# Gate projections of a hybrid decoder layer: tile by tile, and by Strassen's scheme on pairs of column tiles with three of four weight sums made by adding transfers

## The chip, the cores and the metric

The kernel runs on one core of one Trainium2 chip. A core has a matrix engine (TensorE, PE in the profile), a vector engine (VectorE, DVE), a scalar engine (ScalarE, ACT), a general engine (GpSimd, POOL) and a queue engine (SyncE, SP), each with its own instruction stream; transfers run on 16 DMA engines. PE takes a 128x128 weight block and streams columns of the other operand past it; results go to PSUM, eight banks of 128 x 512 fp32. All other tiles lie in SBUF. The metric is device time in microseconds (us); lower is better. Before: 1664.61 us, the median of 3 runs (1664.39 to 1665.62).

## What is computed

One decoder layer on 512 tokens of width 2048, in float32, no batch:

```python
h = rmsnorm(x) * (1 + scale) + shift                  # scale, shift, gate from c @ w_ada
q_lat, kv_lat, k_rope, z_mla, u, v, z_sgu, g_mla, g_sgu = split(h @ w_in)
A = causal_attention(from q_lat, kv_lat, k_rope) * silu(z_mla)
B = u * (tril(W_s) @ rmsnorm(v) + b_s) * silu(z_sgu)   # chunks of 128 tokens
x = x + gate * ((sigmoid(g_mla) * A + sigmoid(g_sgu) * B) @ w_out)
out = rmsnorm(x)
```

The change is about the five projections of width 2048 that gate the two branches: z_mla, g_mla, u, z_sgu, g_sgu, here called types z, g, u, s, t. Each has 16 column tiles of 128, one per head.

## The kernel before

Every product of two fp32 matrices is made of three float32r matmuls: each operand is split into a high part (`hi`, a cast on ACT) and a low part (`lo`, a subtraction on DVE), and `mm3` (L133 to L136) adds hi*hi, hi*lo and lo*hi into one PSUM bank. The input h stands transposed in SBUF as 16 chunks of 128 rows by 512 tokens, as pairs `hh[j]`, `hl[j]`.

Weights come through one `Stream` (L53): granules of up to 128 x 1024 are loaded into three raw buffers in a fixed order (L76, on SP's queue), then split into one of two `whi`/`wlo` pairs (L97 on ACT, L98 on DVE) one granule ahead of their use. Every engine runs its instructions in the order in which the program is written, so the order of the Python calls is the schedule.

The stages, in order: the modulation vectors and the first 1664 columns of the projection (latents, and three gate tiles of head 15 among them); v (L466); the gate projections of heads 0 to 14 (L749); the last two gate tiles of head 15 (L814); attention head by head (L1008); the output projection (L1068).

In the gate stage each head h has five tiles t, each with two granules of eight chunks: 16 chunks of three matmuls over all 512 tokens. After a tile, `evac` (L693) applies the gate from PSUM. Beside that run the spatial mix of v (`sgu_prep`, `sgu_mix`) for the first eight h, the sums that carry `shift` into the early projections (`shift_share`), the rotary tables (`rope_part`, one small step before each granule) and the norms of the latents. The gate results of all 32 tiles stay in SBUF until attention uses them.

## Time and profile before

| | |
|---|---|
| median of 3 runs | 1664.61 us |
| profiled execution, its own time | 1664.88 us |
| its span | 1663.2 us |
| mean granted TensorE clock | 0.999 |
| waits of PE that the profile shows, all together | 3.7 us (1.6 + 1.1 + 0.8 + 0.2) |
| data moved | 228.63 MB, 137 GB/s over the span |

The span is what the profile sees between the first and the last instruction. A PE row's duration is not its cost: matmuls overlap, so the cost of one in a stream is the distance between the starts of two neighbours. Rows of DVE and ACT do not overlap with others of the same engine; their durations add up.

### The profile page before, as it was taken

The page shows a single profiled execution, that of the slowest core. Times are in us where ns is not written, and L with a number is a line of the kernel's source. Part 1 is how long each engine was busy: PE and PEld are TensorE (multiplying, and loading weights), DVE is VectorE, ACT ScalarE, POOL GpSimd, SP SyncE. Part 2 cuts the span into 40 slices and gives each one's busy share as a digit, 9 for nine tenths or more (in the row PEclk, how much of TensorE's full clock was granted, in tenths as well). Part 3 has the DMA queues.
Part 4 walks back from the last instruction along what each step waited for, and adds up shares of the span by engine and source line. Part 5 has one row for each costly group of instructions (what it writes and reads, how often), then busy time and mean ns, then how long its engine had stood idle before and what let it go on. Part 6 is the DMA issues. An engine that isn't in the chain of part 4 may idle for free.

```text
span 1663.2 us, 20082 instructions
## 1 busy us (share of the span) xinstructions
PE 1651.6 (99%) x8024; PEld 1406.1 (85%) x8024; DVE 947.5 (57%) x1456; ACT 583.3 (35%) x967; POOL 2.2 (0%) x11
## 2 busy tenths in 40 slices
PE   9999999999999999999999999999999999999998
PEld 7888889988888888888888888888898888888887
DVE  8988646365665644444443533323578778874453
ACT  4343333234223322221223322222455555542332
POOL 0000000000000000000000000000000000000000
PEclk9999999999999999999999999999999999999999
DMA  9878557344444333322222222232311221126332
GB/s 379 346 295 303 193 211 269 101 151 143 142 152 132 120 137 127 123 102 89 98 92 102 89 101 100 90 102 81 96 61 58 63 75 55 61 77 253 127 101 101
DMA packets 64508, 228.63 MB, mean 137 GB/s; under 512 B 7304, under 2 KB 9376, under 8 KB 57632
## 3 DMA queue, kind: packets, MB, share of 16 engines
q1 hardware_dynamic: 64416, 227.37, 38.7%
q8 instruction: 62, 1.02, 0.2%
q14 instruction: 30, 0.25, 0.0%
HBM read 223.14 MB, written 4.20 MB: 137 GB/s over the span
## 4 chain that ended last, share of the span: by engine, by line
PE 98%; DMA 1%; DVE 0%; ACT 0%; issue 0%; SPq 0%; DVEq 0%
PE ps L135 32%; PE ps L134 32%; PE ps L136 32%; PE ps L947 1%; PE ps L675 1%; PE ps L910 1%; PE ps L911 1%; DMA wraw<-in_w 1%; PE ps L676 0%; DMA wada<-in_c 0%; PE ps L606 0%; DVE wlo L98 0%; ACT whi L97 0%; PE ps L446 0%; DVE wada L122 0%
## 5 line engine op out<-in xcount | busy, mean ns | idle before, releaser
L98 DVE TENSOR_TENSOR wlo<-wraw,whi 128x1024 fp32r<-128x1024 f32 (+3 forms) x304 | 339.0, 1115 | 577.4 <-ACT whi L97 566.4
L134 PE MATMUL ps<-hh,whi 128*128 128x512 f32 x1640 | 641.6, 391 | 0.2 <-ACT hh L389 0.2
L135 PE MATMUL ps<-hl,whi 128*128 128x512 f32 x1640 | 638.5, 389 | 0.8 <-DVE hl L125 0.8
L136 PE MATMUL ps<-hh,wlo 128*128 128x512 f32 x1640 | 638.4, 389 | 0.0
L97 ACT CAST whi<-wraw 128x1024 fp32r<-128x1024 f32 (+3 forms) x304 | 293.7, 966 | 801.6 <-PE ps L135 561.0
L136 PEld LDWEIGHTS ps<-hh,wlo 128*128 128x128 f32 x1640 | 307.8, 188 | 64.5 <-DVE wlo L98 0.2
L135 PEld LDWEIGHTS ps<-hl,whi 128*128 128x128 f32 x1640 | 308.0, 188 | 64.0 <-DVE hl L125 1.1
L134 PEld LDWEIGHTS ps<-hh,whi 128*128 128x128 f32 x1640 | 307.9, 188 | 63.7 <-ACT hh L389 0.6
L134 PE MATMUL ps<-whi,hh 128*128 128x512 f32 (+3 forms) x448 | 148.9, 332 | 0.0
L135 PE MATMUL ps<-wlo,hh 128*128 128x512 f32 (+3 forms) x448 | 148.6, 332 | 0.1
L136 PE MATMUL ps<-whi,hl 128*128 128x512 f32 (+3 forms) x448 | 148.5, 332 | 0.0
L125 DVE SCALAR_TENSOR_TENSOR wada<-wada,cact 128x2048 f32<-128x2048 f32 x47 | 107.2, 2281 | 1.2 <-DMA wada<-in_wada 1.2
L135 PEld LDWEIGHTS ps<-wlo,hh 128*128 128x128 f32 x448 | 84.6, 189 | 5.4 <-DVE wlo L98 0.4
L136 PEld LDWEIGHTS ps<-whi,hl 128*128 128x128 f32 x448 | 84.6, 189 | 5.0
L134 PEld LDWEIGHTS ps<-whi,hh 128*128 128x128 f32 x448 | 84.6, 189 | 5.0
L134 PE MATMUL ps<-whi,b 128*128 128x512 f32 (+1 forms) x212 | 81.8, 386 | 0.0
L135 PE MATMUL ps<-wlo,b 128*128 128x512 f32 (+1 forms) x212 | 81.6, 385 | 0.0
L136 PE MATMUL ps<-whi,g 128*128 128x512 f32 (+1 forms) x212 | 81.6, 385 | 0.0
L134 PEld LDWEIGHTS ps<-whi,b 128*128 128x128 f32 x212 | 39.8, 188 | 7.9
L135 PEld LDWEIGHTS ps<-wlo,b 128*128 128x128 f32 x212 | 39.8, 188 | 7.9
L136 PEld LDWEIGHTS ps<-whi,g 128*128 128x128 f32 x212 | 39.8, 188 | 7.9
L139 ACT CAST lat<-ps 128x512 fp32r<-128x512 f32 (+1 forms) x64 | 35.4, 570 | 13.4 <-PE ps L136 13.3
(229 smaller groups left out, 1340.8 us busy)
## 6 DMA issues: line engine op xcount, KB each, us to landing
wraw<-in_wh SPq DMA_DIRECT2D x150, 512.0 KB, 3.3
wada<-in_wada SPq DMA_DIRECT2D x47, 1024.0 KB, 5.9
wraw<-in_w SPq DMA_DIRECT2D x32, 512.0 KB, 3.5
wraw<-in_wo SPq DMA_DIRECT2D x32, 512.0 KB, 3.3
wraw<-in_w SPq DMA_DIRECT2D x32, 320.0 KB, 2.9
wraw<-in_wv SPq DMA_DIRECT2D x16, 512.0 KB, 3.2
wraw<-in_wv SPq DMA_DIRECT2D x16, 384.0 KB, 3.3
wraw<-in_wq SPq DMA_DIRECT2D x16, 384.0 KB, 2.9
```

Source lines behind the costliest of these rows:

```text
L97: self.nc.scalar.copy(hi[:, :n], raw[:, :n])
L98: self.nc.vector.tensor_tensor(out=lo[:, :n], in0=raw[:, :n], in1=hi[:, :n].bitcast(F32), op=ALU.subtract)
L125: DVE.scalar_tensor_tensor(out=out, in0=in0, scalar=scalar, in1=in1, op0=op0, op1=op1, **kw)
L134: PE.matmul(ps, ah, bh, start=start, stop=False)
L135: PE.matmul(ps, ah, bl, start=False, stop=False)
L136: PE.matmul(ps, al, bh, start=False, stop=stop)
L139: ACT.copy(hi, src)
L675: PE.matmul(ps[:, n2], vh[:, n, :], whl[:, q], start=True, stop=False)
L910: PE.matmul(ps, q2[:, q], krh[:, :n], start=False, stop=False)
L911: PE.matmul(ps, q2[:, q], krl[:, :n], start=False, stop=True)
L947: PE.transpose(ps[:, o:o + P], pr_[i][:, j * P:(j + 1) * P], ident)
```

## The change

The gate projections of 76 of the 77 tiles (all of heads 0 to 13, and of 14 and 15 what is left) are computed in 38 pairs of column tiles (`PAIRS`) by Strassen's scheme in Winograd's form. A pair is a 2x2 block problem: the two halves of the 2048 rows of weights, the two column tiles, and the two halves of the 512 tokens. It takes seven products of eight chunks, each over 256 columns, where two tiles took eight such block products (as 16 chunks over 512 columns, twice). One tile (type z, head 14) is still made plainly.

* Sums of the activations (`s1`, `s2`, `s4`) are made once, during the stage of v; `s3` replaces the right half of `hh[0..7]`, `hl[0..7]` at the start of the gate stage.
* Of a pair's four quarters of weights, called 11, 12, 21 and 22, four sums are needed: 11 += 12 by DVE, then 11 += 22, 12 += 22 and 11 += 21 by transfers from DRAM that add into SBUF, issued on POOL's queue. In the first and the last pair DVE makes one and three of these.
* Each product has its own split into `hi` and `lo`, two products ahead, into one of three buffers. The program is a list of slots, one product each; other work is attached to a slot with `on(slot, phase, ...)`.
* The memory that all this needs is freed by writing v, the latents and the 32 gate results to DRAM and fetching them later: the results during attention (`fetch`, 32 loads of 128 x 512), before the key weights of each head.
* The same side work as before (mix, shift sums, latents, rotary tables) runs inside the slots. Two row sums become one plain fp32 matmul each. PSUM banks are named instead of taken in turn.

```diff
+PAIRS = [((t, h), (t, h + 1)) for h in range(0, 14, 2) for t in TYPES]
+PAIRS[5:5] = [(("g", 14), ("u", 14))]
+PAIRS += [((t, 14), (t, 15)) for t in "st"]
...
+    def make_s12(j):
+        a, b = (nt(tb.p, [P, S], F32, f"t{i}") for i in range(2))
+        tt(a, hh[j].bitcast(F32), hl[j].bitcast(F32), ALU.add)
+        tt(b[:, right], hh[j + 8].bitcast(F32)[:, right], hl[j + 8].bitcast(F32)[:, right], ALU.add)
+        tt(b[:, right], a[:, right], b[:, right], ALU.subtract)
+        split_sum("s1", j, b[:, right])
+        tt(b[:, left], b[:, right], a[:, left], ALU.subtract)
+        split_sum("s2", j, b[:, left])
...
+    for i in range(13):
+        early.setdefault(8 + i, []).append(lambda i=i: lat_scale(i))
+    for j in range(8):
+        early.setdefault(11 + 2 * j + j // 2, []).append(lambda j=j: make_s12(j))
+        early.setdefault(32 + j, []).append(lambda j=j: make_s4(j))
...
+            turn_ = [(1, k), (6, k), (3, k - 1), (7, k), (4, k - 1), (5, k), (2, k)]
...
+    def transfer(t, k, q, add):
+        ty, h = PAIRS[k][q % 10 - 1]
+        eng = dict(accum_op=ALU.add) if add else {}
+        q_ = nc.gpsimd if add else DMA
...
+        if h < H - 1:
+            q_.dma_start(t, wh[h, n, q // 10 - 1], **eng)
+            return
...
+        on(at_[6] - 2, GATE, add, k, 11, 12)
+        for p, q, r, ready in ((2, 11, 22, at_[6]), (3, 12, 22, at_[6]), (4, 11, 21, at_[2])):
+            if acc_[p]:
+                on(ready - 1, LOAD, lambda k=k, q=q, r=r: transfer(raws[k, q], k, r, True))
+            else:
+                on(at_[p] - 2, GATE, add, k, q, r)
...
+    def make_s3(j):
+        a = slot(("rx", "lat12")[j % 2])
+        tt(a, hh[j].bitcast(F32), hl[j].bitcast(F32), ALU.add)
+        tt(a[:, left], a[:, left], a[:, right], ALU.subtract)
+        hilo(hh[j][:, right], hl[j][:, right], a[:, left])
+    for j in range(8):
+        on(-2 + j * 2 // 3, BACK, make_s3, j)
...
+    for i in range(0, len(rope), 2):
+        on(s_ + 4 + i // 2, BACK, lambda i=i: [f() for f in rope[i:i + 2]])
...
-                for k in range(8):
-                    j = half * 8 + k
-                    sl = slice(k * P, (k + 1) * P)
-                    mm3(ps, wH[:, sl], wL[:, sl], hh[j], hl[j], j == 0, j == KC - 1)
...
+    for s, (p, k) in enumerate(order):
+        if s > 0:
+            evacuate(*order[s - 1], s)
+        run(s, FIRST, EVAC, GATE, SPLIT, BACK)
+        begin(p, k)
+        ps, rt_, (wH, wL) = bank_for(p, k), rights[p], split_of.pop(s)
+        for c in range(8):
+            xh, xl = rt_(c)
+            sl = slice(c * P, (c + 1) * P)
+            st, sp = c == 0 and p in (1, 5, 6), c == 7
+            PE.matmul(ps, wH[:, sl], xh, start=st, stop=False, skip_group_check=True)
+            PE.matmul(ps, wH[:, sl], xl, start=False, stop=False, skip_group_check=True)
+            PE.matmul(ps, wL[:, sl], xh, start=False, stop=sp, skip_group_check=True)
+        run(s, MISC, LOAD)
```

How the instructions stand on the engines, at the three places that matter below. First PE, in the middle of the gate stage before (`whi`, `wlo`: a granule's split weights; `hh`, `hl`: the chunks):

```order
L134 MATMUL ps_4983<-hh_173_1384,whi_4950 128x512
L135 MATMUL ps_4983<-hl_175_1388,whi_4950 128x512
L136 MATMUL ps_4983<-hh_173_1384,wlo_4951 128x512
L134 MATMUL ps_4983<-hh_183_1431,whi_4984 128x512
L135 MATMUL ps_4983<-hl_185_1435,whi_4984 128x512
L136 MATMUL ps_4983<-hh_183_1431,wlo_4985 128x512
```

and with the change, where one product ends and the next begins (`s4h`, `s4l`: a sum of activations; `w0`, `w2`: two of the three split buffers):

```order
L1159 MATMUL ps_588_5145<-s4h_2709,w0h_5141 128x256
L1160 MATMUL ps_588_5145<-s4l_2710,w0h_5141 128x256
L1161 MATMUL ps_588_5145<-s4h_2709,w0l_5142 128x256
L1159 MATMUL ps_547_4845<-hh_184_1460,w2h_5172 128x256
L1160 MATMUL ps_547_4845<-hl_186_1464,w2h_5172 128x256
L1161 MATMUL ps_547_4845<-hh_184_1460,w2l_5173 128x256
```

A split of 128 x 1024 now serves 24 matmuls of 256 columns instead of 24 of 512.

Second DVE, where the rotary tables are made; before (`wlo`: low part of a granule; `rb` to `rs`: the table's steps; `acc`: the shift sums):

```order
L98 TENSOR_TENSOR wlo_3147<-wraw_3040,whi_3146 128x1024
L125 SCALAR_TENSOR_TENSOR acc_277_2869<-wraw_3034,shift_91,acc_277_2869 128x1024
L129 TENSOR_SCALAR rd_3155<-rb_2950 128x128
L131 TENSOR_SCALAR re_3157<-rd_3155 128x128
L122 TENSOR_TENSOR rd_3155<-rd_3155,re_3157 128x128
L122 TENSOR_TENSOR rs_3046<-rs_3046,rd_3155 128x128
L98 TENSOR_TENSOR wlo_3187<-wraw_3097,whi_3186 128x1024
```

and with the change (`w0l`, `w2l`: low parts of two successive products; `lat`: a result being gathered from PSUM; `rx`, `cosT`: the table's steps):

```order
L123 TENSOR_TENSOR lat_1251_10439<-lat_1251_10439,ps_1245_10376 128x256
L123 TENSOR_TENSOR w0l_10709<-raw_1259_10528,w0h_10708 128x1024
L130 TENSOR_SCALAR rx_10530<-rx_10530 128x128
L132 TENSOR_SCALAR rx_10530<-rx_10530 128x128
L123 TENSOR_TENSOR rx_10530<-rx_10530 128x128 x2
L130 TENSOR_SCALAR rx_10530<-cosT_10531 128x128
L132 TENSOR_SCALAR rx_10530<-rx_10530 128x128
L123 TENSOR_TENSOR rx_10530<-rx_10530 128x128 x2
L123 TENSOR_TENSOR w2l_10747<-raw_1242_10366,w2h_10746 128x1024
```

Before, one step of the table stands between two splits that are half a tile apart; now two steps stand between two splits that are one product apart, and they come late in the stage, over 22 slots.

Third POOL, which had no transfers; now there are three per pair (`raw_392`: quarter 11 of a pair, `wraw_398`: its 12; behind the bracket the semaphores waited for, DVE's among them):

```order
L596 DMA raw_392_3603<-in_wh 128x1024 [waits DMASW1_49,DVE_49]
L596 DMA wraw_398_3641<-in_wh 128x1024 [waits DMAHW5_49,DMASW3_49]
L596 DMA raw_392_3603<-in_wh 128x1024 [waits DMASW0_49,DVE_49]
L596 DMA wraw_423_3850<-in_wh 128x1024 [waits DMASW4_49,DVE_49]
```

The two adds into 11 wait for DVE to have read what stood there; the split of the product that needs the sum waits for them.

## The prediction

> **What bounds the kernel now.** I read the page's busy times and its chain of waits first, then the busy time by stage, then single rows.

> ```profile
> PE 1651.6 (99%) x8024; PEld 1406.1 (85%) x8024; DVE 947.5 (57%) x1456; ACT 583.3 (35%) x967; POOL 2.2 (0%) x11
> ...
> PE 98%; DMA 1%; DVE 0%; ACT 0%; issue 0%; SPq 0%; DVEq 0%
> ```

> PE is busy for all but 12 us of the span, and the chain that ends last is PE by 98%. A change must shorten PE's stream; what it adds elsewhere costs only where PE comes to wait for it. By stage (columns: stretch, its length, then busy time and instructions of PE, PEld, DVE, ACT and POOL, the granted clock, the DMA engines' share, GB/s):

> ```profile
> core 0: us, PE busy (x) PEld busy (x) DVE busy (x) ACT busy (x) POOL busy (x), PEclk, DMA share, GB/s
> 0.00:99.70 99.70, 96.00 (x481) 80.15 (x482) 86.45 (x114) 44.54 (x63) 2.19 (x11) 1.00 0.88 345
> ...
> 176.00:352.00 176.00, 176.00 (x936) 162.02 (x935) 87.64 (x97) 61.83 (x161) 0.00 (x0) 1.00 0.54 194
> ...
> 393.70:787.00 393.30, 393.30 (x1791) 327.52 (x1790) 210.97 (x343) 114.47 (x137) 0.00 (x0) 1.00 0.38 127
> 787.00:1181.00 394.00, 394.00 (x1748) 326.43 (x1747) 151.93 (x168) 109.99 (x133) 0.00 (x0) 1.00 0.27 93
> ...
> 1214.00:1450.00 236.00, 236.00 (x1368) 209.68 (x1367) 188.65 (x404) 126.87 (x281) 0.00 (x0) 1.00 0.20 63
> ```

> The two rows from 393.70 to 1181 are the gate stage. PE is busy throughout; DVE for 211 of 393 us in its first half, 152 of 394 in its second. PE's stream can shrink there before DVE becomes the bound, but by less than half.

> **What the products cost.** Start to start, three matmuls of 512 columns in the gate stage:

> ```profile
> 1183.08 0.39 PE L134 MATMUL ps<-hh,whi 128*128 128x512 f32 x1
> 1183.31 0.39 PE L135 MATMUL ps<-hl,whi 128*128 128x512 f32 x1
> 1183.54 0.39 PE L136 MATMUL ps<-hh,wlo 128*128 128x512 f32 x1
> 1183.76 0.39 PE L134 MATMUL ps<-hh,whi 128*128 128x512 f32 x1
> ```

> 0.68 us for three, 0.2267 each, so a tile of 48 takes 10.88 us. Matmuls of 256 columns, each with its own weight block, already stand in the values' projection of attention:

> ```profile
> 1204.04 0.28 PE L136 MATMUL ps<-whi,hl 128*128 128x256 f32 x1
> 1204.16 0.28 PE L134 MATMUL ps<-whi,hh 128*128 128x256 f32 x1
> ...
> 1209.44 0.28 PE L136 MATMUL ps<-whi,hl 128*128 128x256 f32 x1
> ```

> 45 steps in 5.40 us: 0.120 us each. It is more than half of 0.2267, so Strassen's seven eighths do not come out whole. A slot of 24 takes 2.88 us, a pair of seven 20.16 us where two tiles took 21.76. Removed: 76 tiles x 10.88 = 826.9 us. Added: 38 x 7 = 266 slots x 2.88 = 766.1 us. **PE's stream shrinks by 60.8 us**; the spatial mix and the one plain tile stay as they are.

> [...]

> **DVE, slot by slot.** Durations, of the same shapes, from the groups by line:

> ```profile
> L98 DVE TENSOR_TENSOR wlo<-wraw,whi 128x1024 fp32r<-128x1024 f32 x216 | 264.5, 1225 | 505.9 <-ACT whi L97 495.8 <-PE ps L676 9.7
> L97 ACT CAST whi<-wraw 128x1024 fp32r<-128x1024 f32 x216 | 227.7, 1054 | 690.4 <-PE ps L135 526.4 <-PE ps L136 89.0 <-issue 54.3
> ...
> L122 DVE TENSOR_TENSOR b<-b,sig 128x512 f32<-128x512 f32 x32 | 21.9, 685 | 1.4 <-ACT sig L712 0.7 <-ACT sig L707 0.7
> ...
> L125 DVE SCALAR_TENSOR_TENSOR b<-ps,vec,tmp 128x256 f32<-128x256 f32 x32 | 15.5, 484 | 1.1
> ...
> L125 DVE SCALAR_TENSOR_TENSOR lat<-lat,bias,rq 128x512 f32<-128x512 f32 x6 | 4.5, 744 | 0.0
> ...
> L131 DVE TENSOR_SCALAR re<-rd 128x128 f32<-128x128 f32 x16 | 3.6, 228 | 0.5
> ...
> L122 DVE TENSOR_TENSOR rd<-rd,re 128x128 f32<-128x128 f32 x12 | 3.5, 293 | 0.4
> ...
> L122 DVE TENSOR_TENSOR whl<-wsr,whl 128x256 fp32r<-128x256 f32 x8 | 3.4, 426 | 3.8 <-ACT whl L139 3.8
> L215 DVE RECIPROCAL rq<-rq 128x512 f32<-128x512 f32 x1 | 3.4, 3354 | 0.7 <-ACT rq L214 0.7
> ```

> An ordinary pair gives DVE seven low parts (7 x 1.225), one add of 128x1024 that I price like a low part (1.225), three gathers from PSUM of 256 columns (0.42 each, between the 0.426 and 0.484 rows) and 2.4 gate operations (0.685): 12.7 of 20.16 us. ACT has seven casts of 1.054 and copies and sigmoids, some 10 us. With all side work, the 266 slots hold 266 low parts (326), 42 adds (51), 125 operations of 512 columns (86), 112 gathers (47), 57 shift sums and norms (43), 64 steps of the mix (31) and some 65 us of small rows: 649 of 766 us, 85%. So DVE fits on the whole but not everywhere. A low part stands two slots ahead of its product, so it may be late by at most 5.8 us counted from its slot's start; I added DVE's rows in their new order against that limit. PE waits at these places:

> * The opening. Eight makings of `s3` (0.685 + 2 x 0.42 = 1.53 each) and the first pair's adds fall on the first slots: 23.9 us of DVE where six slots give 17.3. I take 8 us of waiting, bounds 3 and 11.
> * The rotary tables. They were one step per granule of 2.72 us of half a tile; now two steps stand in each slot of 2.88. Four parts of 18 scalar rows (0.228), 13 of 0.293 and a few more make 35 us in 22 slots. In the 21 busiest DVE has 76 us of work and 60.5 us of room; less the 2.5 us of lead that it brings, 13 us. Bounds 8 and 18.
> * Single slots: a reciprocal of 3.35 us behind a split, twice, and the mix, whose four steps of 0.484 meet an add and a split in one slot at every second head and wait about 1 us for PE's own mix matmuls. 7 us, bounds 2 and 12.

> Before the gate stage, `make_s12` (0.685 + 5 x 0.42 = 2.8) and the scaling of the latents come into the stage of v, whose granules last

> ```profile
> 249.76 0.33 PE L134 MATMUL ps<-whi,hh 128*128 128x384 f32 x1
> ...
> 253.92 0.33 PE L134 MATMUL ps<-whi,hh 128*128 128x384 f32 x1
> ```

> 4.16 us, beside these:

> ```profile
> L125 DVE SCALAR_TENSOR_TENSOR wada<-wada,cact 128x2048 f32<-128x2048 f32 x47 | 107.2, 2281 | 1.2 <-DMA wada<-in_wada 1.2
> ...
> L98 DVE TENSOR_TENSOR wlo<-wraw,whi 128x768 fp32r<-128x768 f32 x40 | 38.2, 956 | 33.8 <-ACT whi L97 33.0
> ```

> In one granule dot, scaling, `s12` and split make 2.28 + 0.69 + 2.8 + 0.96 = 6.7 us plus two waits for ACT's casts; three more touch the limit. DVE was busy for 88 of 176 us there. 2 us, bounds 0 and 5.

> **Small terms.** From the chain of waits:

> ```profile
> 99.75 0.86 PE ps L446 x2
> ...
> 919.78 0.23 PE ps L209
> ...
> 1200.99 0.46 issue
> 1201.45 1.07 ACT whi L97
> 1202.54 1.24 DVE wlo L98
> 1203.82 0.39 PE ps L135
> ```

> The fp32 row sum at 99.75 takes 0.86 us; the two row sums of latents become of that kind, where each was two matmuls of 0.23: +0.8 us. The last four rows are the handover to attention, where PE stood idle for 0.4 us behind a cast and a low part. Now two of the latents' splits and the last gathers can only follow the last product, while the first attention products (18 matmuls of 0.2267, 4.1 us) cover them: 2 us, bounds 0 and 6.

> **Transfers.** Rows of issue to landing:

> ```profile
> wraw<-in_wh SPq DMA_DIRECT2D x150, 512.0 KB, 3.3
> wada<-in_wada SPq DMA_DIRECT2D x47, 1024.0 KB, 5.9
> ```

> No adding transfer is in the trace. It reads 512 KB from DRAM and the 512 KB where it adds; bounds are the plain 512 KB load (3.3 us) and, as a nearest row above, the 1 MB load (5.9 us); I take the latter. An add into 11 is issued when the split before has been read, some 0.6 us into the next slot, and its sum is cast four slots after that: 11 us of cover; 12 has more. Plain loads stand six slots ahead. Costed at nothing: the work that hides them is four products; with the cover gone each would cost its time to landing.

> The engines' load: 0.38 of the share for 127 GB/s means 334 GB/s at full share, 1.57 us for 512 KB. A pair has four plain loads (6.3 us) and three adds (3.1 us each if read twice: 9.4): 15.7 of 20.16 us, more in the slots of the shift sums. [...]

> Stores of v and of the latents wait on SP's queue for ACT and DVE in the stage of v; three raw buffers, 12 us of granules, hide that. In attention 32 loads of 256 KB and their waits come onto SP's queue before the key weights. The DMA share there is 0.20 and weights are three granules ahead: nothing; if a wait held the queue for the whole cover, some 3 us per head.

> **The sum.** The profiled run took 1664.88 us (span 1663.2), 0.3 above the median. 1664.9 - 60.8 + 0.8 + (8 + 13 + 7 + 2 + 2) = 1636.9: **1637 us**, with the lower bounds (13) 1618, with the upper (52) 1657.

> **Rivals.**

> *Adding transfers become the bound (slower).* The place is the DMA engines and POOL's queue. With four loads of 1.57 us, three adds fit a pair only up to (20.16 - 6.3) / 3 = 4.6 us each; above that each further us costs 3 x 36 = 108 us. From 4.9 us on the gain is gone. At 5.9 us of all engines' time (if the 1 MB row's landing were occupancy) a pair takes 24.0 us: +3.8 x 36 = 138, less the 25 us of DVE's waits that vanish in it: about 1750. For it: nothing in the trace shows how fast the add is. Against: bytes alone give 3.1 us.

> *DVE becomes the bound throughout.* Its rows may stretch beside twice the transfers and POOL's queue. From 766 / 649 = 1.18 on DVE sets every slot. At 1.25 the 266 slots take 811 us instead of 766 and 28 us of waits: 1637 + 17 = 1654; at 1.27 the gain is gone, at 1.30 (844 us) it is 1687. Against: the 1024-wide low part takes the same time at the start, at a DMA share of 0.88 (the first row by stage), as on the average of all stages:

> ```profile
> L98 DVE TENSOR_TENSOR wlo<-wraw,whi x17: 825/1226/1226, 10.2 to 94.9; 128x1024 fp32r<-128x1024 f32 x16, 128x640 fp32r<-128x640 f32 x1
> ```

> *DVE's waits are hidden better.* If casts and low parts fill the gaps and the lead builds up, only 0 to 10 us of waits stay: 1605 to 1615, say 1608.

> **How the numbers follow.** Forecast 0.52; adding transfers the bound 0.24; DVE the bound 0.16 (0.07 still faster, 0.02 the same, 0.07 slower); waits hidden 0.08. Faster by over 0.2% (3.3 us, what a measurement of this kernel can tell from no change): 0.52 + 0.08 + 0.07 = 0.67. Same 0.03, with 0.01 of the transfers' case. Slower 0.30. The range that holds 8 in 10 leaves out most of the transfers' case: 1606 to 1686; the forecast's own is 1618 to 1657.

> **What would show it.** Right: steps of 0.120 us within a product; PE's waits in the gate stage behind DVE low parts, crowded at its opening and in some 20 slots late in it, and some 30 us in all; adding transfers landing within 8 us. Wrong: PE waiting behind casts that wait for POOL's transfers, DMA share near 1, or low parts well above 1225 ns.

## The result

The changed kernel took 1669.84 us, the median of 6 runs (1668.90 to 1674.57), beside 1664.53 us (1663.97 to 1665.62) for the kernel before: a ratio of 1.0036 with a 95% interval of 1.0023 to 1.0049. It is slower by some 5 us, where the prediction had 1637 us. The profiled execution is the slowest of the six: 1674.57 us, span 1672.8 us, mean granted clock 0.986.

The busy times and the shares of the chain that ended last, on the page of the changed kernel:

```profile
PE 1614.9 (97%) x10760; PEld 1503.1 (90%) x10760; DVE 1203.1 (72%) x1840; ACT 767.0 (46%) x1272; POOL 103.7 (6%) x127
...
PE 79%; DVE 9%; DMA 6%; ACT 3%; issue 2%; SPq 0%; DVEq 0%; ACTq 0%
```

PE's share of the chain fell from 98% to 79%: PE now waits, and behind DVE, DMA and ACT alike. Its busy time fell by 36.7 us only, not by the 60.8 less 0.8 of the shorter stream. So two things came in: waits, and matmuls that take longer. The waits of PE from 350 to 1200 us (engine and line, what it waited for, then us in total, times, longest):

```profile
PE ps L1159 <- ACT lat L717: 13.7, 3, 10.9
PE ps L1159 <- DVE lat L123: 9.2, 5, 3.4
PE ps L1161 <- DVE w2l L123: 4.3, 6, 1.0
...
PE ps L1159 <- ACT w2h L616: 3.3, 2, 2.3
PE ps L1159 <- ACT sinT L1004: 2.5, 1, 2.5
```

One wait of 10.9 us is by far the longest; L717 is the copy of product 6 out of PSUM. PE's timeline in an undisturbed product, and in the product behind that wait:

```profile
420.12 0.28 PE L1159 MATMUL ps<-hh,w1h 128*128 128x256 f32 x1
420.24 0.28 PE L1160 MATMUL ps<-hl,w1h 128*128 128x256 f32 x1
```

```profile
373.40 0.41 PE L1159 MATMUL ps<-s4h,w1h 128*128 128x256 f32 x1
373.61 0.41 PE L1160 MATMUL ps<-s4l,w1h 128*128 128x256 f32 x1
373.83 0.41 PE L1161 MATMUL ps<-s4h,w1l 128*128 128x256 f32 x1
```

0.120 us a step in the first, 0.213 in the second. The windows around that wait tell why (length, then busy time and instructions of PE, PEld, DVE, ACT and POOL, granted clock, DMA share, GB/s):

```profile
360.00:362.00 2.00, 1.03 (x9) 0.82 (x7) 0.04 (x1) 1.97 (x4) 0.00 (x0) 1.00 0.46 90
362.00:364.00 2.00, 0.00 (x0) 0.00 (x0) 1.02 (x1) 0.94 (x2) 0.00 (x0) 1.00 0.00 0
364.00:366.00 2.00, 0.00 (x0) 0.00 (x0) 1.50 (x4) 0.40 (x1) 0.00 (x0) 0.50 0.00 0
...
372.00:374.00 2.00, 2.00 (x9) 2.00 (x10) 1.22 (x2) 0.74 (x1) 0.00 (x0) 0.50 0.00 0
376.00:378.00 2.00, 2.00 (x12) 2.00 (x12) 1.49 (x4) 0.41 (x1) 0.72 (x1) 0.58 0.95 337
378.00:380.00 2.00, 2.00 (x19) 2.00 (x18) 0.97 (x4) 1.35 (x2) 0.00 (x0) 1.00 0.45 97
```

PE stops at 361.0, and from 364 on the granted clock is 0.50. It stays there for 5.7 us after PE has resumed at 371.95. DMA is idle (share 0.00) in that wait, so it is not a transfer that PE's releaser is late for.

**The account of the profiled execution.** Without waits it would take 1664.9 - 60.8 + 0.8 = 1604.9 us; it took 1674.6, which is 69.7 more. From the starts of neighbouring matmuls, counting each distance that is over 0.25 us longer than the step (the profile's idle time is some 0.16 us less for each wait, since a matmul's row ends after its step): waits of 3.2 us in the stage of v and 49.0 us from 345 to 1240 us. From windows of 2 us in that same stretch, busy time times what the clock lacks of 1: 13.9 us at half clock. Together 66.1 of the 69.7; the rest is spread thinly. In place of one missing term there are 20 us more of waits than the 32 forecast, and 14 us of a kind that the forecast did not have.

The times below are of the gate stage by stretch, from the first matmul of one product to that of another, in each run's trace. Products 0 to 8 hold the makings of `s3` (the opening), 28 to 155 the shift sums, 155 to 204 the late gates and the latents, 204 to 236 the rotary tables and the end of the latents.

| us between products | 0-8 | 8-28 | 28-155 | 155-204 | 204-236 | 236-265 | sum |
|---|---|---|---|---|---|---|---|
| changed kernel | 39.1 | 59.8 | 377.7 | 161.8 | 117.3 | 85.0 | 840.7 |
| without adding transfers | 39.0 | 59.8 | 374.7 | 148.6 | 115.4 | 85.0 | 822.7 |
| waits filled with matmuls | 38.0 | 59.8 | 378.1 | 160.0 | 115.8 | 85.0 | 836.7 |
| `s3` spread | 37.5 | 61.4 | 377.6 | 160.4 | 115.8 | 85.0 | 837.6 |
| `s3` spread, cast later | 29.3 | 59.8 | 375.6 | 159.0 | 115.8 | 85.0 | 824.4 |
| rotary tables in halves | 38.5 | 59.8 | 376.7 | 159.5 | 106.5 | 85.0 | 826.0 |
| latents in three places | 38.6 | 59.8 | 377.8 | 153.3 | 117.2 | 85.0 | 831.7 |
| these three together | 29.3 | 59.8 | 376.2 | 156.2 | 97.6 | 85.0 | 804.1 |
| and further edits | 27.8 | 59.8 | 376.6 | 149.9 | 97.5 | 85.0 | 796.7 |

### The profile page after: what moved, and what is told of

Same layout as the page of the kernel before. It is cut to its first block, busy times and chain, and to the rows that moved or that the text cites. A ratio compares the mean times of both kernels' runs of the same rounds, so it can differ in the third digit from the quotient of the medians.

```text
span 1672.8 us, 27059 instructions
## 1 busy us (share of the span) xinstructions
PE 1614.9 (97%) x10760; PEld 1503.1 (90%) x10760; DVE 1203.1 (72%) x1840; ACT 767.0 (46%) x1272; POOL 103.7 (6%) x127
## 3 DMA queue, kind: packets, MB, share of 16 engines
q1 hardware_dynamic: 99008, 269.72, 46.0%
q0 software_dynamic: 17728, 57.68, 19.9%
## 4 chain that ended last, share of the span: by engine, by line
PE 79%; DVE 9%; DMA 6%; ACT 3%; issue 2%; SPq 0%; DVEq 0%; ACTq 0%
PE ps L136 14%; PE ps L137 14%; PE ps L135 14%; PE ps L1159 11%; PE ps L1161 11%; PE ps L1160 11%; DMA rx<-lat_d 2%; DMA latn_d<-rx 1%; DVE lat L123 1%; DVE w2l L123 1%; PE ps L1321 1%; DVE w0l L123 1%; DVE rx L123 1%; DVE w1l L123 1%; PE ps L1284 1%
## 5 line engine op out<-in xcount | busy, mean ns | idle before, releaser
L1159 PE MATMUL ps<-hh,w2h 128*128 128x256 f32 x400 | 115.8, 289 | 8.1 <-DVE lat L123 5.6
L1159 PE MATMUL ps<-hh,w0h 128*128 128x256 f32 x416 | 118.9, 286 | 3.5 <-DVE lat L123 3.5
L1161 PE MATMUL ps<-hh,w0l 128*128 128x256 f32 x416 | 118.3, 284 | 1.0 <-DVE w0l L123 1.0
L1160 PE MATMUL ps<-hl,w0h 128*128 128x256 f32 x416 | 118.4, 285 | 0.0
L1161 PE MATMUL ps<-hh,w2l 128*128 128x256 f32 x400 | 115.1, 288 | 1.8 <-DVE w2l L123 1.8
L1160 PE MATMUL ps<-hl,w2h 128*128 128x256 f32 x400 | 114.8, 287 | 0.0
L1159 PE MATMUL ps<-hh,w1h 128*128 128x256 f32 x400 | 113.9, 285 | 0.0
L1161 PE MATMUL ps<-hh,w1l 128*128 128x256 f32 x400 | 113.4, 284 | 0.1
L1160 PE MATMUL ps<-hl,w1h 128*128 128x256 f32 x400 | 113.3, 283 | 0.0
L126 DVE SCALAR_TENSOR_TENSOR wada<-wada,cact 128x2048 f32<-128x2048 f32 x47 | 107.1, 2281 | 0.0
L123 DVE TENSOR_TENSOR w2l<-raw,w2h 128x1024 fp32r<-128x1024 f32 x56 | 68.4, 1222 | 37.2 <-ACT w2h L616 37.1
L136 PE MATMUL ps<-w0l,hh 128*128 128x256 f32 (+3 forms) x288 | 93.3, 324 | 1.9 <-DVE w0l L106 1.9
L135 PE MATMUL ps<-w0h,hh 128*128 128x256 f32 (+3 forms) x288 | 93.6, 325 | 0.9 <-ACT w0h L105 0.9
L135 PE MATMUL ps<-hh,w1h 128*128 128x512 f32 x226 | 90.4, 400 | 0.2 <-ACT hh L378 0.2
L136 PE MATMUL ps<-hl,w1h 128*128 128x512 f32 x226 | 88.9, 393 | 0.8 <-DVE hl L126 0.8
## 6 DMA issues: line engine op xcount, KB each, us to landing
raw<-in_wh SPq DMA_DIRECT2D x105, 512.0 KB, 7.1
wada<-in_wada SPq DMA_DIRECT2D x47, 1024.0 KB, 7.2
wraw<-in_wh POOLq DMA_DIRECT2D x66, 512.0 KB, 7.1
wraw<-in_wh SPq DMA_DIRECT2D x45, 512.0 KB, 7.6
raw<-in_wh POOLq DMA_DIRECT2D x42, 512.0 KB, 7.1
wraw<-in_wo SPq DMA_DIRECT2D x32, 512.0 KB, 3.7
wraw<-in_w SPq DMA_DIRECT2D x16, 512.0 KB, 8.5
wraw<-in_wv SPq DMA_DIRECT2D x16, 512.0 KB, 4.8
```

Source lines behind the costliest of these rows:

```text
L123: DVE.tensor_tensor(out=out, in0=in0, in1=in1, op=op)
L126: DVE.scalar_tensor_tensor(out=out, in0=in0, scalar=scalar, in1=in1, op0=op0, op1=op1, **kw)
L135: PE.matmul(ps, ah, bh, start=start, stop=False)
L136: PE.matmul(ps, ah, bl, start=False, stop=False)
L1159: PE.matmul(ps, wH[:, sl], xh, start=st, stop=False, skip_group_check=True)
L1160: PE.matmul(ps, wH[:, sl], xl, start=False, stop=False, skip_group_check=True)
```

## The experiments

Theories: T1, DVE and ACT are late where work is crowded, and TensorE's clock is halved after each longer wait. T2, the adding transfers make the waits. T3, the clock falls for another reason than waits. T4 came out of the third run: ACT and DVE wait for each other in turn.

### The adding transfers left out

```diff
-                on(ready - 1, LOAD, lambda k=k, q=q, r=r: transfer(raws[k, q], k, r, True))
+                pass
```

> Leaves out the 110 adding transfers; three of the four weight sums of a pair are then missing from the output. Theory T1 (DVE and ACT rows are late at the opening, at the rotary tables and at the latents, and TensorE's clock is halved after each longer wait): the DVE rows are unchanged, so the 13 us of waits at the opening and the 17 us among the rotary tables stay; only the waits behind round trips to DRAM shrink. 1664 to 1674 us, against 1669.8 with the transfers. Theory T2 (the adding transfers, by the traffic or by POOL's queue, make the waits): PE's waits in the gate stage fall from 49 us to 20 or less and the clock stays up: 1630 to 1645.

Measured: 1654.95 us (ratio to before 0.9939, interval 0.9924 to 0.9954), 15 us less than the changed kernel: between the two. The opening and the rotary tables stayed (39.0 and 115.4 us), as T1 has it. The gain is in the stretch of the late gates and the latents (13.2 us) and in that of the shift sums (3.0 us), more than T1 gave them. Transfer rows (engine, count, KB each, median us from issue to landing) of the changed kernel, with its two queues (packets, MB, share of 16 engines):

```profile
raw<-in_wh SPq DMA_DIRECT2D x105, 512.0 KB, 7.1
...
wraw<-in_wh POOLq DMA_DIRECT2D x66, 512.0 KB, 7.1
```

```profile
q1 hardware_dynamic: 99008, 269.72, 46.0%
q0 software_dynamic: 17728, 57.68, 19.9%
```

The same plain loads without the adding transfers:

```profile
raw<-in_wh SPq DMA_DIRECT2D x105, 512.0 KB, 4.3
```

An adding transfer lands in 7.1 us in the median and the slowest in 11.6, the slowest into a quarter 11 in 10.8, just within the cover of 11; no wait that the profile shows in the gate stage ends with one. It makes the plain 512 KB loads of the gate stage beside it slower (4.3 to 7.1 us), and where DVE waits in order for a tile that comes from DRAM, PE feels it: DVE's waits for such loads of the gate stage's side work (the raw tiles of the shift sums, latents and gates that come back) sum to 34.0 us in the changed kernel and to 0.9 us without the adding transfers.

### The waits filled with matmuls

```diff
+FILL = {2: 48, 160: 14, 184: 15, 219: 12, 226: 11, 232: 10}
...
+        if s in FILL:
+            spare = bank_at(w_bank)
+            for _ in range(FILL[s]):
+                PE.matmul(spare, hh[8][:, :P], hh[9], start=True, stop=True, skip_group_check=True)
```

> Adds 110 matmuls of 512 columns on old data (24.9 us of PE at 0.2267) in front of six products, as many as fit the wait that the trace shows there (10.9, 3.2, 3.4, 2.7, 2.5 and 2.3 us); nothing reads their result. T1 (a wait of more than some 2 us halves the clock): the clock stays at 1.00 through the opening and behind the two waits among the latents, those products take 2.9 us again instead of 5.3 to 5.5, and the kernel is 4 to 10 us faster, though it does more; among the rotary tables little is won, since DVE sets the time there. T3 (the clock falls for another reason, the stream of 256 columns or the load of all engines): the half clock stays in those places and the kernel is 0 to 15 us slower.

Measured: 1669.47 us (ratio 1.0032, interval 1.002 to 1.0045). The first window of half clock in the opening, in this run:

```profile
364.00:366.00 2.00, 2.00 (x10) 1.65 (x10) 1.49 (x4) 0.41 (x1) 0.00 (x0) 1.00 0.00 0
...
372.00:374.00 2.00, 2.00 (x19) 2.00 (x18) 0.89 (x2) 1.05 (x1) 0.00 (x0) 1.00 0.35 51
```

The granted clock is 1.00 where it was 0.50, and so it is behind the other five filled waits; three new stretches at half clock stand at products 195, 225 and 230, behind shorter waits that were not filled. The half clock from 345 to 1240 us fell from 13.9 to 6.8 us of PE's time, and product 2 took 2.96 us instead of 5.29. That speaks for T1 and against T3 for the clock. But the time hardly moved: 24.9 us of added matmuls cost nothing, and the 4 to 10 us expected of the clock did not come. From product 3 to product 8 it took 15.9 us instead of 14.6: PE, no longer slow, waited for ACT and DVE instead. Where those set the time, the half clock is free; the changed kernel's 14 us at half clock are an upper bound on its price, not the price.

### The makings of `s3` spread, alone

```diff
-        on(-2 + j * 2 // 3, BACK, make_s3, j)
+        on(-2 + j, BACK, make_s3, j)
```

> Spreads the eight makings of s3 one to a slot over slots -2 to 5 (eight slots instead of five); their first user is slot 7. T1: the copy that product 7 waits for no longer stands behind five makings on ACT, the 11 us wait before slot 2 falls to 3 or less, the half clock behind it goes, and 10 to 16 us are won: 1654 to 1660. T2: the opening has one adding transfer only, and the wait is due to transfers of raw weights: 0 to 3 us.

Measured: 1668.19 us (ratio 1.0025, interval 1.0016 to 1.0034), a miss: the wait before product 2 is still 9.0 us, though fewer makings stand ahead of it. ACT's timeline there (in brackets the idle time before, and what ended it):

```profile
360.24 0.40 ACT L140 CAST hh<-rx 128x256 fp32r<-128x256 f32 x1 [2.35 <-DVE rx L123]
360.55 0.37 ACT L714 COPY lat<-ps 128x256 f32<-128x256 f32 x1
360.81 1.05 ACT L616 CAST w0h<-raw 128x1024 fp32r<-128x1024 f32 x1
364.21 0.40 ACT L140 CAST hh<-lat 128x256 fp32r<-128x256 f32 x1 [2.35 <-DVE lat L123]
364.52 0.37 ACT L717 COPY lat<-ps 128x256 f32<-128x256 f32 x1
```

ACT is idle for 2.35 us ahead of each cast of a making, because that cast waits for DVE's two sums, which stand behind the low part of the slot's weights on DVE, which in turn waits for ACT's cast of these weights. The copy that PE needs (L717) stands behind the cast. Neither engine is full; they take turns. That is T4, and it is in the chain of waits of the changed kernel too:

```profile
362.01 0.94 ACT w1h L616
362.98 1.22 DVE w1l L123
364.20 0.61 DVE lat L123
364.84 0.44 DVE lat L123
365.30 0.41 ACT hh L140
365.73 0.42 DVE hl L123
...
371.63 0.28 ACT lat L717
371.95 0.58 PE ps L1159
```

One turn with one making is 0.94 + 1.22 + 0.61 + 0.44 + 0.41 = 3.6 us, more than a slot of 2.88, while DVE's own rows in it are 2.7.

### The makings spread, and their casts one slot later

```diff
-        hilo(hh[j][:, right], hl[j][:, right], a[:, left])
+        on(done[0] + 1, BACK, hilo, hh[j][:, right], hl[j][:, right], a[:, left])
...
-        on(-2 + j * 2 // 3, BACK, make_s3, j)
+        on(-2 + j, MISC, make_s3, j)
```

> As the run that spreads the makings of s3 one to a slot, and the cast and low part of each making are put one slot later, behind that slot's split. Theory T4: ACT and DVE each work in order and wait for each other in turn (cast, low part, two sums, cast: 1.05 + 1.23 + 0.61 + 0.44 + 0.41 = 3.74 us to a slot of 2.88), so the opening is bound by this chain, not by DVE's 23.9 us of rows. With the cast put later ACT's next split waits for nothing on DVE: the two waits of 9.1 and 2.3 us that were left in the opening fall to 4 us or less in all, with the half clock behind them: 1654 to 1661. If instead DVE's rows alone bound the opening, the wait stays near 8 us and the time at 1665 to 1668.

Measured: 1660.15 us (ratio 0.9973, interval 0.9963 to 0.9982), 9.7 us less than the changed kernel with the same rows on both engines. The wait before product 2 is down to

```profile
360.57 0.38 PE L1159 MATMUL ps<-s4h,w1h 128*128 128x256 f32 x1 [2.39 <-ACT lat L717]
```

and two further ones before product 8 are 1.7 and 1.2 us: 5.3 us in all, a little over the 4 expected, with the time inside its range. T4 holds for the opening: 8.2 us more come from putting the cast and the low part of a making one slot later than from spreading the work (37.5 to 29.3 us in the table). The edit also puts the two sums behind the slot's other work on DVE; that was not run by itself.

### The rotary tables in halves

```diff
-        w = S // 4
+        w = S // 2
...
-    for part in range(4):
+    for part in range(2):
...
-        rt.append(slot("rx"))
+        rt.append(nt(mis.p, [P, GW], F32, "raw3"))
...
-    for i in range(0, len(rope), 2):
-        on(s_ + 4 + i // 2, BACK, lambda i=i: [f() for f in rope[i:i + 2]])
+    for i in range(len(rope)):
+        on(s_ + 4 + i, BACK, rope[i])
```

> The rotary tables in two parts of 256 columns instead of four of 128, with the raw buffer of the shift sums as room, and one step to a slot instead of two; the slots are the same 22. Their rows take some 24 us of DVE instead of 35. T1: the 17 us of waits and the 5 us or so of half clock between 1000 and 1100 us of the trace fall to 6 or less, 10 to 17 us are won: 1653 to 1660. T2: the waits there are from transfers, and less than 4 us are won.

Measured: 1658.70 us (ratio 0.9967, interval 0.9955 to 0.998), 11 us less, as T1 had it. Windows from product 216 to 236, of the changed kernel and of this run:

```profile
1026.48:1108.40 81.92, 66.93 (x497) 64.54 (x498) 66.38 (x158) 42.82 (x65) 7.77 (x9) 0.94 0.63 158
```

```profile
1020.70:1092.60 71.90, 63.55 (x498) 61.38 (x497) 57.08 (x104) 38.46 (x58) 7.71 (x9) 0.98 0.71 180
```

DVE has 9.3 us less to do and the stretch is 10.0 us shorter. PE is still idle for 8.4 us, where T1 expected 6 or less of waits and half clock together, and ACT's timeline of this run shows one reason:

```profile
1078.05 0.42 ACT L1011 ACTIVATE cosT<-raw 128x256 f32<-128x256 f32 x1 [2.61 <-DVE raw L132]
1078.37 0.35 ACT L717 COPY lat<-ps 128x256 f32<-128x256 f32 x1
```

A sine waits 2.6 us for DVE's step of the same slot, and the next copy out of PSUM stands behind it: T4 again.

### The latents read back into three places

```diff
-        lat_in[i] = slot(("rx", "sinT")[n % 2])
+        lat_in[i] = nt(mis.p, [P, GW], F32, "raw3")[:, :S] if n % 3 == 2 else slot(("rx", "sinT")[n % 3])
```

> The latents are read back into three places in turn instead of two (the third is the free raw buffer of the shift sums), so a load no longer waits for the store from the same place that was issued one slot before. T1 with the round trips to DRAM as one of its waits: the waits of 3.3 us near 847 and 3.5 us near 924 of the trace fall below 1 us each and the half clock behind them goes: 8 to 12 us won, 1658 to 1662. If the waits there are from the adding transfers' traffic itself and not from the two places, less than 3 us are won.

Measured: 1662.51 us (ratio 0.9991, interval 0.9982 to 1.0), 7.3 us less: short of the 8 to 12 expected, and well over the 3 of the other reading. The chain of waits of the changed kernel here:

```profile
895.81 8.97 DMA latn_d<-rx
...
904.79 2.97 DMA rx<-lat_d
...
908.84 7.28 DMA latn_d<-rx
...
916.14 7.09 DMA rx<-lat_d
```

A normed latent leaves `rx` for DRAM (7.3 us), then the next one comes into it (7.1 us): 14.4 us, five slots, where the program leaves four. With a third place the wait near 924 is gone, as expected; the one near 847 is still 1.9 us, from 3.3, because there the gate that comes back into `cosT` waits for a store from `cosT`.

### All three together, and the rest

> All of these together: makings of s3 spread and their casts put later, rotary tables in two parts of 256 columns with one step to a slot and the sine one slot behind its argument, latents read into three places. If the gains add up (some 10 at the opening, 11 at the rotary tables, 10 at the latents): 1636 to 1645, faster than both kernels. If a wait that is removed only turns up at the next place, 1650 or more.

Measured, with the sine also one slot behind its argument: 1634.68 us (ratio 0.9829, interval 0.9815 to 0.9842), just under the range expected. The gains add up, and a little over: 35 us, where the three alone gave 9.7, 11.1 and 7.3. By the table the opening's gain comes through whole, that at the latents in part (5.6 of 8.5 us), and the rotary tables gain more (106.5 to 97.6 us); there the sine's place is what no run had before, though it was not run by itself.

The next kernel mends the places that its trace still showed:

```diff
+            junk = nt(latp.p, [P, S], F32, "lat11") if cg == 4 else nt(tb.p, [P, S], F32, "sig", bufs=2)
...
+        on(-3 + j, MISC, make_s3, j)
...
+            ss["u"] = nt(mis.p, [P, S], F32, "r3b")
...
+    gate_op("z", 14, gate_src, 3)
...
+        for q, half in enumerate((left, right)):
+            on(done[0] + 1 + q, MISC, lambda half=half: DVE.reciprocal(out=ss[0][:, half], in_=ss[0][:, half]))
...
+    for i in (6, 7, 8, 9):
+        lat_split(i)
```

> On top of the run that puts the three edits together: makings of s3 one slot earlier, one sigmoid of the opening later, the last stores of v from two buffers in turn, the raw buffer of the shift sums as two tiles (one of them for the gate that comes back from DRAM), the reciprocal of the latents in two halves, and four of the latents' splits behind the first attention weights. The run before had 20 us of waits and some 8 us of half clock left. T4 (ACT and DVE wait for each other in turn, and every longer wait halves the clock): waits fall to 10 us and the half clock to 3: 1618 to 1628. If the waits that go only move to the next place, 1632 or more.

Measured: 1628.50 us (ratio 0.9783, interval 0.9769 to 0.9798), half a microsecond above what was expected: 2.2% faster than the kernel before and 41 us faster than the change as it came. The window of the rotary tables, products 216 to 236, in which PE now waits for 2.5 us:

```profile
1000.90:1063.80 62.90, 60.37 (x498) 59.62 (x497) 55.88 (x104) 35.98 (x55) 7.71 (x9) 1.00 0.79 200
```

Waits are 15.4 us from 345 to 1240 us, where 10 were expected, the half clock is 1.6 us, and the mean granted clock is 0.996 with the same stream of 256 columns: nothing is left of T3. The next run is the same kernel without its adding transfers.

> The same without the 110 adding transfers (three of the four weight sums of a pair are missing from the output). The first run without them was 15 us faster than the changed kernel. T1: that was by the latents' round trips, which waited for landings of 7 us instead of 4, and the half clock behind them; with these places mended the adding transfers cost 5 us or less. T2: they slow other work too, and 10 us or more are won by leaving them out.

Measured: 1622.85 us (ratio 0.975, interval 0.9734 to 0.9767), 5.6 us less than with the transfers, a little over T1's 5. So most of the first 15 us went through the places that are mended now (T1). What is left lies in the stretch of the shift sums (1.9 us) and that of the latents (3.1 us), where loads are used three slots after their issue.

### The sums by DVE instead

```diff
-        return {2: k > 0 and k < n_pairs - 1, 3: k < n_pairs - 1, 4: k < n_pairs - 1}
+        return {2: n_pairs - 2 <= k < n_pairs - 1, 3: n_pairs - 2 <= k < n_pairs - 1, 4: n_pairs - 2 <= k < n_pairs - 1}
```

> 107 of the 110 adding transfers become adds of 128x1024 on DVE (1.225 us each, 131 us in all), each ahead of the cast that reads its sum. By DVE's rows alone: 649 + 131 = 780 us for slots of 766 us, so DVE is the bound by little: 1605 + 14 and some 60 us of waits and half clock as now, 1670 to 1700. T4 (ACT and DVE in turn): in four of a pair's seven slots the add stands behind the last low part and in front of the next cast, 1.15 + 1.05 + 1.23 = 3.43 us to the slot, in the other three 2.28, and with gathers (1.2) and gate operations (1.6) a pair takes 23.4 us instead of 20.16: 36 x 3.2 = 115 us more, 1740 to 1800.

Measured: 1872.15 us (ratio 1.1251, interval 1.1232 to 1.127), beyond both. Its chain of waits:

```profile
617.31 1.14 DVE wraw L123
...
618.55 1.06 ACT w0h L616
...
620.77 1.23 DVE wraw L123
...
622.02 3.64 DMA raw<-in_wh
...
625.74 1.06 ACT w1h L616
```

The turns of T4 are there (add, cast, low part), but a third thing stands between them: a DVE add needs its second summand in SBUF for six slots longer (product 3 or 4 of a pair against 7 or 5), its buffer is single, and the next pair's load is issued late: 3.6 us of the chain here. The adding transfer saves not only DVE's 1.2 us; it holds no buffer. How the 202 us divide between turns and late loads was not measured.

## Why the prediction was wrong

By the profiled run the forecast is short by 37.7 us (1674.6 for 1636.9): 20.2 us more of waits than the 32 forecast, 13.9 us at half clock, and 3.6 us that were not traced to a place.

**The stream of PE: right.** Steps of 0.120 us, products of 2.88 us (206 of the 266 took under 2.95). In the last kernel the 1604.9 us without waits, its 15.4 us of waits and its 1.6 us of half clock make 1621.9 of the 1628.50 measured, so the 60.8 us are there to within 7 us. That the 1634.68 us of an earlier mended kernel lie near the forecast 1637 is chance: its waits are other ones than those forecast.

**The opening, 8 us [3 to 11]: the step that failed.** "I added DVE's rows in their new order against that limit": that takes DVE for the only engine in line. The rows were right (1.53 us a making, 1.225 a low part), though rows of DVE and ACT do overlap by a little, so that their sums are somewhat high: at 362.98 us of the changed kernel a low part of 1.22 us is followed by a sum that starts at 364.12, 0.08 us before its end, and the rows of ACT above overlap by 0.09. What sets the slot is the turn through both engines, 3.6 us instead of 2.7. The waits came to 13.2 us, above the upper bound, and one slot more between the sums and their cast took 8.2 us off the opening at the same DVE work. The 8 itself had no working: 23.9 less 17.3 us leaves 6.6.

**The rotary tables, 13 us [8 to 18]: right in cause and in range.** 17.5 us of waits from product 216 to 232; half of the rows' count and, in the kernel with all three edits, the sine one slot later took the stretch from 117.3 to 97.6 us. The 35 us of rows are there (35.1), but the "granule of 2.72 us" is 5.44 us in the trace before, half of a tile's 10.88: the steps became nearly four times as dense, not twice. The sum does not use it. The sine's turn was the part not seen.

**Single slots, 7 us [2 to 12]: above the range, and mostly by another cause.** The waits are 13.0 us from 540 to 990 us. Without the adding transfers 2.8 us of them stay, so the reciprocals and the mix that the term was made of cost at most that; the rest went with the transfers, and lies mostly behind latents and gates that come back from DRAM.

**Transfers, "Costed at nothing": the other step that failed, by a path that it left out.** The rates were right: 19.9% of 16 engines over 1672.8 us is 333 us for 110 sums, 3.0 us each, where 3.1 was taken; the median landing is 7.1 us, though 45 of the 108 of 512 KB took more than the 8 us named. But only the weights' cover was checked. The loads that other work waits for (three to four slots ahead, some behind a store from the same place) had no such cover; leaving the adding transfers out won 15 us, the largest gain of any single edit.

**The stage of v, 2 us, and the handover, 2 us:** 3.2 and 4.2 us, both within their bounds. The 0.4 us of idle time that the prediction reads at the handover before are 0.06 us by PE's rows there; the 0.39 us in the chain's last row are a matmul.

**The clock: no term at all.** Seven waits of 2.1 us and more, six in the gate stage and one at the handover, are each followed by half clock, 13.9 us in all. Its price is less, as the filled waits show.

**The rivals.** Adding transfers as the bound: no. From 610 to 830 us PE is full at a clock of 1.00, beside a DMA share of 0.88:

```profile
610.00:830.00 220.00, 220.00 (x1835) 219.77 (x1835) 165.40 (x218) 107.78 (x164) 27.43 (x32) 1.00 0.88 235
```

DVE the bound throughout by longer rows: no, the low part of 128x1024 stayed at 1222 ns:

```profile
L123 DVE TENSOR_TENSOR w2l<-raw,w2h 128x1024 fp32r<-128x1024 f32 x56 | 68.4, 1222 | 37.2 <-ACT w2h L616 37.1
```

The end of this row says it too: DVE was idle for 37.1 us ahead of these 56 low parts, waiting for ACT's casts, though ACT is at 46%. Waits hidden better: no.

## What to carry to other kernels

Where two in-order engines feed each other within a step, cost the step by the chain through both (3.6 us here), not by the larger sum (2.7); a cast that waits for the other engine belongs one step later, behind the work that doesn't wait (8.2 us of the opening here). A transfer that is itself in time still costs what it adds to the landings beside it (7.1 us for 4.3 here): look for loads with a short lead, above all those that come into a place just stored from (7.3 us out and 7.1 in here). Cutting an engine's stream by some 4% is worth that much only while every step beside it still fits the shorter step.

## What was not expected of the hardware

```profile
845.30:848.71 3.41, 0.93 (x5) 0.73 (x6) 1.71 (x2) 3.41 (x6) 0.19 (x1) 1.00 0.64 182
848.71:852.12 3.41, 3.41 (x18) 3.41 (x17) 3.32 (x5) 1.42 (x3) 1.54 (x2) 0.50 0.60 89
```

PE was idle for 2.5 us of the first, and the second is at half clock, though PE is busy throughout. Counted so in the eleven traces from 345 to 1240 us (to 1400 in the longest), all 50 windows that were at full clock with over 1.8 us of idle time (seven of them in the changed kernel) were followed by half clock, 12 of 34 with 1.45 to 1.8 us, and none with less. The wait of 2.8 us that passed was divided between two windows. In the changed kernel the least idle of the seven, 1196.87 to 1200.28 us, had PE idle for 1.96 of its 3.41 us, so there a window idle by somewhat over half was enough.

**A half clock that costs little.** From product 204 to 236 the changed kernel had three spells of half clock and took 117.3 us; without the adding transfers it had one and took 115.4, of which 1.5 lie behind the last of these waits. Between them PE waited for DVE and ACT in either run.

**An adding transfer costs the engines about twice a plain one.** By the queues it is 57.68 MB in 19.9% of the span's engine time against 269.72 MB in 46.0%: 0.345% and 0.171% per MB. By what the engines are spared when the adding transfers are left out (65.9% of 1672.8 us against 48.6% of 1653.5 us for the two queues) it is 2.7 us each, 1.7 times the 1.56 us that 512 KB of plain transfers take there.
